# GpSimd forms the low halves of the query weights and of the first ten streamed blocks in a hybrid encoder kernel

## The chip, the core and the metric

The kernel runs on one core of one Trainium2 chip. The metric is the device time of one execution in microseconds (us); lower is better. The time before is the median of three runs.

## The reference, cut to what matters

One encoder block over 512 tokens of width 1024: a mixer (short convolution and pooling) with its output projection, then an expert retrieval with product keys, then a gated input embedding and a last norm. The change lies in the expert retrieval:

```python
def peer_block(xb, w_q, sub_keys, expert_u, expert_v):
    q = (xb @ w_q).reshape(T, PEER_HEADS, 2, PEER_HALF)      # 8 heads, 2 x 128
    s = jnp.einsum('thpd,hpkd->thpk', q, sub_keys)           # 128 keys per half
    sv, si = lax.top_k(s, PEER_TOPK)                         # 16 of 128
    cand = sv[:, :, 0, :, None] + sv[:, :, 1, None, :]       # 256 candidates
    top_s, pos = lax.top_k(cand, PEER_TOPK)                  # 16 of 256
    eidx = jnp.take_along_axis(cidx, pos, axis=-1)           # 16384 experts
    gate = jax.nn.softmax(top_s, axis=-1)
    act = jax.nn.gelu(jnp.einsum('thkd,td->thk', expert_u[eidx], xb))
    return jnp.einsum('thk,thkd->td', gate * act, expert_v[eidx])
```

## The kernel before

**Products of split numbers.** Most matmuls are done in three passes. A float32 operand is split into a high half, a rounded copy that ScalarE writes, and a low half, the remainder, which is a subtraction of two tiles in SBUF. `mm3` and `mm3_pair` then issue high x high, high x low and low x high. `split_ld` (lines 95 to 97) makes both halves, for weight pieces in `piece` (lines 166 to 170: load of 128x2048, high half `wH`, low half `wL`), and `projT` (lines 172 to 177) uses them for a projection onto 256 columns.

**Query stage (lines 498 to 520).** For each of 8 heads `projT` makes the queries of 512 tokens from one piece of `w_q`; the piece of the next head is prepared meanwhile in the other of two buffers (line 501). The scores against the keys go to the tile `s`, and VectorE takes the top 16 of each half there and then (`head`, lines 340 to 352).

**Dense and gathered experts.** For 384 of the 512 tokens the kernel doesn't gather: it streams all 16384 rows of `expert_u` in 128 blocks, multiplies each with all tokens and weights the results by a gate matrix that is zero nearly everywhere. The other 128 tokens (group `ND`) use gathers: GpSimd issues 256 indirect DMAs of 128 rows (`fetch`, lines 534 to 538) and VectorE does the arithmetic (`gather`, lines 545 to 567). Gathers need the indices `eidx` (line 436).

**Block loop (lines 614 to 640).** For block `i` of 76: SP issues the load of block `i + 2` into one of two buffers `uraw` (`u_dma`), ScalarE makes its high half `uH` (`u_h`), VectorE its low half `uL` (`u_l`, lines 582 to 586), three buffers each; TensorE scores block `i` in 24 matmuls of 384 columns; ScalarE applies the gelu, and every fourth block a write `A_d` goes to memory. `prep_u` gives both halves a high priority. Beside this, `main` holds the rest of the retrieval as a list of tasks for VectorE, group `ND` first: candidates, second top-k, decoding of the positions, softmax, `eidx`; then for the other three groups the same and the one-hot products that build the gate matrix, written out as `G_d`. The loop places the tasks in proportion to the blocks done, and gathers from block `G_START` = 10 on at 0.7 per block.

**Order.** From line 237 to line 751 a planner orders the instructions of each engine: it simulates them by priority and by its own estimate of their durations. Line 563 pins the gathers' arithmetic in program order. The first stage and everything from line 752 on (the mixing of `expert_v`) run in the order written.

Of the kernel before, what the change touches and what calls it, by code (L numbers as in the profile page):

```python
# [7 lines left out]
F32 = mybir.dt.float32  # L8
# [5 lines left out]
OP = mybir.AluOpType  # L14
# [34 lines left out]
GGB = 2  # L49
URB = 2  # L50
G_START = 10
G_RATE1 = 0.7
RATES = (1.5, 3.2, 2.9)
MAIN_ORDER = ((ND, 0, 99), (0, 0, 99), (1, 0, 99), (2, 0, 99))
# [6 lines left out]
def block_kernel(ctx: ExitStack, tc: tile.TileContext, x, pT_in, g_cols, w_in, conv_w, pool_w,  # L61
                 pool_scale, w_o, g_ffn, w_q, keysT, u_rows, u_blk, v_rows, g_ple, w_gate, w_proj,
                 g_final, inv_cnt, iota_rep, iota_c, ident_in, out):
    nc = tc.nc
# [27 lines left out]
    gate3 = consts.tile([P, P], F32, name="gate3")  # L92
    xrow = consts.tile([P, D], F32, name="xrow")

    def split_ld(src, hi, lo):
        nc.scalar.activation(hi, src, AF.Copy)
        nc.vector.tensor_tensor(lo, src, hi.bitcast(F32), op=OP.subtract)

    def rsqrt(ms):
        sq = small.tile([P, 1], F32, name="sq")  # L100
# [57 lines left out]
    def piece_dma(w, c0):  # L158
        raw = wpool.tile([P, DC, 256], F32, name="wraw")
        nc.sync.dma_start(raw, w[:, c0:c0 + 256].rearrange("(c p) n -> p c n", p=P))  # L160
        return raw

    def piece_hl():
        return (wpool.tile([P, DC, 256], F32R, name="wH"), wpool.tile([P, DC, 256], F32R, name="wL"))

    def piece(w, c0):
        raw = piece_dma(w, c0)
        hl = piece_hl()
        split_ld(raw, *hl)
        return hl  # L170

    def projT(w, xh, xl):
        ps = [psum.tile([P, T], F32, name="acc", bufs=4) for _ in range(2)]
        for c in range(DC):
            mm3_pair([(ps[b], w[0][:, c, b * P:(b + 1) * P], w[1][:, c, b * P:(b + 1) * P], xh[:, c], xl[:, c])
                      for b in range(2)], c == 0, c == DC - 1)
        return ps
# [18 lines left out]
    pieces = {}  # L196
# [29 lines left out]
    for c in range(DC + LEAD):  # L226
        if c < DC:
            split_ld(raw0[:, c], w0[0][:, c], w0[1][:, c])
            xT_chunk(0, xs, xh, xl, c)
        d = c - LEAD  # L230
        if d >= 0:
            split_ld(raw1[:, d], w1[0][:, d], w1[1][:, d])
            for b in range(2):
                s = slice(b * P, (b + 1) * P)
                mm3(first[b], w0[0][:, d, s], w0[1][:, d, s], xh[:, d], xl[:, d], d == 0, d == DC - 1)
# [36 lines left out]
    for k, pc in enumerate(order):  # L272
        w = pieces.pop(pc)
        if 0 < k < len(order) - 1:
            pieces[order[k + 1]] = piece(w_in, order[k + 1] * 256)
        elif k:
            pieces["o0"] = piece(w_o, 0)
        both = projT(w, xh, xl) if k else first
        for b in range(2):
            ps = both[b]  # L280
            blk = 2 * pc + b
            kind, g = divmod(blk, 4)
            if kind == 3:
                pool_group(g, ps)
            elif kind == 1:
                cbuf[g] = wk.tile([P, T], F32, name="cb")
                nc.scalar.activation(cbuf[g], ps, AF.Copy)
            elif kind == 2:
                z = wk.tile([P, T + 2], F32, name="zb", bufs=1)
                nc.vector.memset(z[:, 0:1], 0.0)  # L290
                nc.vector.memset(z[:, T + 1:], 0.0)
                nc.vector.tensor_tensor(z[:, 1:T + 1], cbuf[g], ps, op=OP.mult)
                y = wk.tile([P, T], F32, name="yb")
                nc.vector.tensor_scalar(y, z[:, 0:T], cw[:, g, 0:1], None, op0=OP.mult)
                nc.vector.scalar_tensor_tensor(y, z[:, 1:T + 1], cw[:, g, 1:2], y, op0=OP.mult, op1=OP.add)
                nc.vector.scalar_tensor_tensor(y, z[:, 2:T + 2], cw[:, g, 2:3], y, op0=OP.mult, op1=OP.add)
                zbuf[g] = y
            else:
                m = wk.tile([P, T], F32, name="cm", bufs=1)
                nc.vector.tensor_tensor(m, zbuf[g], ps, op=OP.mult)  # L300
                split_ld(m, mixH[:, g], mixL[:, g])

    corder = [4, 5, 6, 7, 0, 1, 2, 3]
    for qd in range(4):
        w = pieces.pop("o%d" % qd)
        if qd < 3:
            pieces["o%d" % (qd + 1)] = piece(w_o, (qd + 1) * 256)
        else:
            pieces["q0"] = piece(w_q, 0)
        for t in range(NT):  # L310
            ps = psum.tile([P, T], F32, name="acc", bufs=4)
            ts = slice(t * P, (t + 1) * P)
            for ci, c in enumerate(corder):
                mm3(ps[:, :256], mixH[:, c, ts], mixL[:, c, ts], w[0][:, c], w[1][:, c], ci == 0, ci == DC - 1)
            hs = h[:, t, qd * 256:(qd + 1) * 256]
            nc.vector.tensor_tensor(hs, hs, ps[:, :256], op=OP.add)
# [181 lines left out]
    for hd in range(H):  # L498
        w = pieces.pop("q%d" % hd)
        if hd + 1 < H:  # L500
            pieces["q%d" % (hd + 1)] = piece(w_q, (hd + 1) * 256)
        qb = []
        both = projT(w, xh, xl)
        for b in range(2):
            ps = both[b]
            qs = wk.tile([P, T], F32, name="cb" if b else "yb")
            nc.scalar.activation(qs, ps, AF.Copy)
            qb.append(qs)
        sh_ = wk.tile([P, NT, 2, P], F32, name="s", bufs=3)
        for tp in range(2):  # L510
            ps = psum.tile([P, T], F32, name="tp", bufs=2)
            for ti in range(2):
                for b in range(2):
                    t = 2 * tp + ti
                    o = (2 * ti + b) * P
                    nc.tensor.matmul(ps[:, o:o + P], qb[b][:, t * P:(t + 1) * P], keys[:, 2 * hd + b],  # L516
                                     start=True, stop=True)
            nc.scalar.activation(sh_[:, 2 * tp:2 * tp + 2],
                                 ps.rearrange("p (t b k) -> p t b k", t=2, b=2), AF.Copy)
        for t in (ND, 0, 1, 2):  # L520
            heads[t](hd, sh_[:, t])
# [23 lines left out]
    def gather(n=1, pin=False):  # L545
        for _ in range(n):
            k = done[0]
            if k >= 2 * P:
                return
            done[0] += 1  # L550
            for kk in range(k, min(k + AHEAD_G, 2 * P)):
                if kk not in rows:
                    rows[kk] = fetch(u_rows if kk < P else v_rows, kk % P)
            g = rows[k]
            if k < P:
                ins = nc.vector.scalar_tensor_tensor(g, g, 1.0, xrow, op0=OP.mult, op1=OP.mult,  # L556
                                                     accum_out=act[:, k:k + 1])
            else:
                accg = accs["g"]
                ins = nc.vector.scalar_tensor_tensor(accg, g, gate3[:, k - P:k - P + 1], accg, op0=OP.mult,  # L560
                                                     op1=OP.add)
            if pin:
                tc.keep_in_program_order(ins)
            if k == P - 1:
                nc.sync.dma_start(xrow, h_d[ND])
                nc.scalar.activation(act, act, AF.Gelu_apprx_tanh)
                nc.vector.tensor_tensor(gate3, gate3, act, op=OP.mult)

    ublk, vblk, wblk = {}, {}, {}
# [12 lines left out]
    def u_l(i):  # L582
        if i < NE:
            raw, uh, _ = ublk[i]
            ublk[i][2] = ub.tile([P, DC, P], F32R, name="uL")
            nc.vector.tensor_tensor(ublk[i][2], raw, uh.bitcast(F32), op=OP.subtract)  # L586

    def v_dma(n):
        if n < NE:
# [28 lines left out]
    def prep_u(i):  # L618
        u_dma(i)
        with tc.high_priority(AHEAD):  # L620
            u_h(i)
            u_l(i)
# [3 lines left out]
    for i in range(NB):  # L626
# [9 lines left out]
        while mi < len(main) and spent < (i + 1) * total_m / (NB - SLACK):  # L636
            spent += main[mi][0]
            main[mi][1]()
            mi += 1
        gather(max(0, int((i + 1 - G_START) * G_RATE1) - done[0]), True)  # L640
    phg.close()
# [64 lines left out]
    def quota(r):  # L706
        rate[0] += r
        n = int(rate[0])
        rate[0] -= n
        return n  # L710
# [61 lines left out]
    for m in range(PRE):  # L772
        heldU[m] = acts(NR + m)
        if m == 0:
            for t in range(ND):
                acc[t] = [psum.tile([P, T], F32, name="o%d%d" % (t, hf)) for hf in range(2)]
        u_h(NB + m + 2)
        u_l(NB + m + 2)
        u_dma(NB + m + 4)
        gelu(NR + m, heldU[m])  # L780
    LAST = 3
    left = None
    for n in range(NE - LAST):
        m = n + LAG
        i = n - NS
# [10 lines left out]
        q = quota(r)  # L796
# [23 lines left out]
        if fu:  # L820
            u_l(u_of(m) + 2)
            u_dma(u_of(m) + 4)
# [168 lines left out]
```

## Time and profile before

| what | value |
|---|---|
| median of three runs | 1458.21 us (1457.02 to 1458.67) |
| the profiled execution | 1454.53 us |
| its span on the core | 1452.8 us |
| TensorE busy | 1429.9 us |
| VectorE busy | 1146.7 us |
| ScalarE busy | 621.5 us |
| GpSimd busy | 385.6 us |

The stages by time in the profiled execution: the mixer to about 160 us, the query stage to 278 us, the streamed blocks of the loop to about 650 us, the mixing to about 1400 us, then the tail. "Busy" is the time in which an engine has an instruction in work. A view by stretches gives the same for any part of the span, with the clock that TensorE was granted (1.00 is 2.4 GHz). A view of waits says who waited for whom. Times inside the span count from its start.

### The profile page before, as it was taken

What the parts mean: (1) busy time and instruction counts of PE and PEld (TensorE: products, weight loads), DVE (VectorE), ACT (ScalarE), POOL (GpSimd) and SP (SyncE); (2) the same over time, 40 slices, a digit from 0 to 9 for tenths busy, and PEclk for the clock granted to TensorE, in tenths of its full rate; (3) what the DMA queues carried; (4) which work ended last, traced back from release to release, by engine and by line L of the source; (5) the groups of instructions that cost most, each with busy time, mean ns of one, the idle gap of its engine ahead of it and who ended that gap; (6) DMA issues with size and microseconds to landing.
All of it is one profiled execution on the core that took longest, in us unless ns stands there. A gap on an engine that the chain in (4) does not pass through costs nothing.

```text
span 1452.8 us, 20735 instructions
## 1 busy us (share of the span) xinstructions
PE 1429.9 (98%) x7785; PEld 1270.7 (87%) x7785; DVE 1146.7 (79%) x2206; ACT 621.5 (43%) x928; POOL 385.6 (27%) x260
## 2 busy tenths in 40 slices
PE   8999999999998999999999999999999999999997
PEld 5789888999998999997999999999998888888886
DVE  5644579899998887877999788887887778777765
ACT  5321533344564665663333333333333334443354
POOL 0000000002132132123766555454453112343000
PEclk9999999999999999999999999999999999999999
DMA  8233630047688899898999989998988899998622
GB/s 302 87 94 104 237 117 30 30 166 275 227 286 275 262 316 328 269 312 292 381 351 357 380 321 334 349 346 326 348 318 281 322 341 343 339 336 329 250 69 73
DMA packets 152086, 381.40 MB, mean 263 GB/s; under 512 B 10929, under 2 KB 72113, under 8 KB 151729
## 3 DMA queue, kind: packets, MB, share of 16 engines
q1 hardware_dynamic: 72400, 211.75, 41.3%
q0 software_dynamic: 36864, 134.23, 25.2%
q10 hardware_dynamic: 42720, 34.08, 7.3%
q8 instruction: 61, 1.00, 0.3%
q14 instruction: 41, 0.33, 0.1%
HBM read 339.92 MB, written 40.11 MB: 262 GB/s over the span
## 4 chain that ended last, share of the span: by engine, by line
PE 79%; DVE 7%; issue 5%; DMA 5%; ACT 1%; POOL 1%; ACTq 0%; SPq 0%; POOLq 0%; DVEq 0%
PE o L125 13%; PE o L127 13%; PE o L123 13%; PE acc L125 7%; PE acc L123 7%; PE acc L127 7%; PE u L127 5%; PE u L123 5%; PE u L125 5%; DMA uraw<-in_u_blk 3%; DVE uL L586 2%; DMA G_d<-stage 1%; PE acc L191 1%; POOL gr L536 1%; PE tp L516 1%
## 5 line engine op out<-in xcount | busy, mean ns | idle before, releaser
L536 POOL DMA_INDIRECT gr<-in_u_rows,eidx x128 | 191.5, 1496 | 664.9 <-DVE tsm L390 334.3
L536 POOL DMA_INDIRECT gr<-in_v_rows,eidx x128 | 193.9, 1514 | 279.8 <-DVE xrow L560 270.7
L125 PE MATMUL o<-vL,wH 128*128 128x512 f32 x768 | 237.2, 390 | 1.0 <-DVE vL L604 1.0
L123 PE MATMUL o<-vH,wH 128*128 128x512 f32 x768 | 237.5, 390 | 0.0
L127 PE MATMUL o<-vH,wL 128*128 128x512 f32 x768 | 237.3, 390 | 0.2 <-DVE wL L684 0.2
L123 PE MATMUL acc<-xH,uH 128*128 128x384 f32 x608 | 206.6, 340 | 3.1 <-ACT uH L580 3.1
L598 ACT ACTIVATE vH<-vraw 128x1024 fp32r<-128x1024 f32 x128 | 135.3, 1057 | 168.5 <-PE o L127 94.5
L125 PE MATMUL acc<-xL,uH 128*128 128x384 f32 x608 | 206.8, 340 | 0.0
L127 PE MATMUL acc<-xH,uL 128*128 128x384 f32 x608 | 204.7, 338 | 0.6 <-DVE uL L586 0.6
L604 DVE TENSOR_TENSOR vL<-vraw,vH 128x1024 fp32r<-128x1024 f32 x128 | 156.1, 1220 | 44.5 <-ACT vH L598 44.4
L580 ACT ACTIVATE uH<-uraw 128x1024 fp32r<-128x1024 f32 x128 | 135.2, 1057 | 103.0 <-DMA uraw<-in_u_blk 63.1
L586 DVE TENSOR_TENSOR uL<-uraw,uH 128x1024 fp32r<-128x1024 f32 x128 | 155.7, 1218 | 23.6 <-ACT uH L580 23.6
L125 PEld LDWEIGHTS o<-vL,wH 128*128 128x128 f32 x768 | 144.0, 188 | 32.6 <-DVE vL L604 1.8
L127 PEld LDWEIGHTS o<-vH,wL 128*128 128x128 f32 x768 | 143.9, 188 | 31.3 <-DVE wL L684 1.0
L560 DVE SCALAR_TENSOR_TENSOR xrow<-gr,gate,xrow 128x1024 f32<-128x1024 f32 x128 | 163.6, 1278 | 4.2 <-DMA xrow<-h_d 4.1
L123 PEld LDWEIGHTS o<-vH,wH 128*128 128x128 f32 x768 | 143.3, 188 | 26.7 <-ACT wH L680 0.2
L556 DVE SCALAR_TENSOR_TENSOR gr<-gr,xrow 128x1024 f32<-128x1024 f32 x128 | 155.1, 1217 | 3.7 <-DMA gr<-in_u_rows,eidx 3.6
L127 PE MATMUL u<-xH,uL 128*128 128x384 f32 x416 | 139.6, 336 | 0.0
L123 PE MATMUL u<-xH,uH 128*128 128x384 f32 x416 | 139.5, 335 | 0.0
L125 PE MATMUL u<-xL,uH 128*128 128x384 f32 x416 | 139.3, 335 | 0.0
L123 PEld LDWEIGHTS acc<-xH,uH 128*128 128x128 f32 x608 | 115.2, 189 | 4.2 <-ACT uH L580 4.1
L127 PEld LDWEIGHTS acc<-xH,uL 128*128 128x128 f32 x608 | 115.0, 189 | 1.4 <-DVE uL L586 1.3
(214 smaller groups left out, 2368.1 us busy)
## 6 DMA issues: line engine op xcount, KB each, us to landing
uraw<-in_u_blk SPq DMA_DIRECT2D x128, 512.0 KB, 4.9
vraw<-in_v_rows SPq DMA_DIRECT2D x128, 512.0 KB, 6.0
G_d<-stage ACTq DMA_DIRECT2D x12, 1664.0 KB, 11.2
gq<-G_d SPq DMA_DIRECT2D x26, 768.0 KB, 7.3
A_d<-a ACTq DMA_DIRECT2D x17, 768.0 KB, 5.3
aq<-A_d SPq DMA_DIRECT2D x17, 768.0 KB, 9.3
wraw<-in_w_in SPq DMA_DIRECT2D x8, 1024.0 KB, 5.8
wraw<-in_w_q SPq DMA_DIRECT2D x8, 1024.0 KB, 5.8
```

What stands on the lines that cost most here:

```text
L123: nc.tensor.matmul(ps, lh, rh, start=start, stop=False)
L125: nc.tensor.matmul(ps, lh, rl, start=False, stop=False)
L127: nc.tensor.matmul(ps, ll, rh, start=False, stop=stop)
L191: nc.tensor.matmul(ps, pT[:, c, t * P:(t + 1) * P], wp[hf][:, c], start=c == 0, stop=c == 1)
L516: nc.tensor.matmul(ps[:, o:o + P], qb[b][:, t * P:(t + 1) * P], keys[:, 2 * hd + b], start=True, stop=True)
L536: nc.gpsimd.indirect_dma_start(out=g, out_offset=None, in_=table, in_offset=bass.IndirectOffsetOnAxis(ap=eidx[:, k:k + 1], axis=0))
L556: ins = nc.vector.scalar_tensor_tensor(g, g, 1.0, xrow, op0=OP.mult, op1=OP.mult, accum_out=act[:, k:k + 1])
L560: ins = nc.vector.scalar_tensor_tensor(accg, g, gate3[:, k - P:k - P + 1], accg, op0=OP.mult, op1=OP.add)
L580: nc.scalar.activation(ublk[i][1], ublk[i][0], AF.Copy)
L586: nc.vector.tensor_tensor(ublk[i][2], raw, uh.bitcast(F32), op=OP.subtract)
L598: nc.scalar.activation(vblk[n][1], vblk[n][0], AF.Copy)
L604: nc.vector.tensor_tensor(vblk[n][2], raw, vh.bitcast(F32), op=OP.subtract)
```

## The change

`split_ld` and `piece` take an engine as an argument. In the query stage the low halves of the pieces of heads 1 to 7 are formed by GpSimd in place of VectorE, and so are those of streamed blocks 0 to 9. Nothing else is edited; the planner orders the instructions anew.

```diff
+UPOOL = 10
...
-    def split_ld(src, hi, lo):
+    def split_ld(src, hi, lo, eng=None):
         nc.scalar.activation(hi, src, AF.Copy)
-        nc.vector.tensor_tensor(lo, src, hi.bitcast(F32), op=OP.subtract)
+        (eng or nc.vector).tensor_tensor(lo, src, hi.bitcast(F32), op=OP.subtract)
...
-    def piece(w, c0):
+    def piece(w, c0, eng=None):
         raw = piece_dma(w, c0)
         hl = piece_hl()
-        split_ld(raw, *hl)
+        split_ld(raw, *hl, eng)
         return hl
...
-            pieces["q%d" % (hd + 1)] = piece(w_q, (hd + 1) * 256)
+            pieces["q%d" % (hd + 1)] = piece(w_q, (hd + 1) * 256, nc.gpsimd)
...
-            nc.vector.tensor_tensor(ublk[i][2], raw, uh.bitcast(F32), op=OP.subtract)
+            (nc.gpsimd if i < UPOOL else nc.vector).tensor_tensor(ublk[i][2], raw, uh.bitcast(F32), op=OP.subtract)
```

## Rows read from the trace of the kernel before

Abbreviations: PE is TensorE, PEld its weight loads, DVE VectorE, ACT ScalarE, POOL GpSimd, SPq the queue from which SP issues DMAs.

**Rows 1.** The page's first part: busy us, share of the span, instructions.
```profile
PE 1429.9 (98%) x7785; PEld 1270.7 (87%) x7785; DVE 1146.7 (79%) x2206; ACT 621.5 (43%) x928; POOL 385.6 (27%) x260
```

**Rows 2.** Busy time by stretches: stretch, length, busy (instructions), clock, DMA share, GB/s.
```profile
186.00:276.00 90.00, 90.00 (x450) 75.37 (x449) 79.23 (x454) 26.92 (x36) 0.00 (x0) 1.00 0.16 52
282.00:334.00 52.00, 52.00 (x302) 52.00 (x301) 52.00 (x252) 24.11 (x32) 0.00 (x0) 1.00 0.50 167
340.00:438.00 98.00, 96.98 (x674) 94.74 (x672) 94.67 (x225) 55.19 (x88) 23.86 (x15) 1.00 0.79 265
438.00:480.00 42.00, 37.34 (x253) 35.03 (x251) 36.77 (x49) 22.18 (x40) 10.49 (x7) 0.92 0.86 274
480.00:700.00 220.00, 218.26 (x1523) 205.53 (x1523) 182.79 (x215) 130.85 (x220) 59.31 (x40) 1.00 0.89 299
700.00:1400.00 700.00, 700.00 (x3360) 613.28 (x3359) 561.37 (x709) 263.21 (x363) 287.66 (x191) 1.00 0.89 328
```
The five busy times stand for PE, PEld, DVE, ACT and POOL, in this order.

**Rows 3.** Timeline of PE at 260 us: start, duration, what, idle before.
```profile
260.44 0.63 PE L125 MATMUL acc<-xL,wH 128*128 128x512 f32 x2
260.90 0.63 PE L127 MATMUL acc<-xH,wL 128*128 128x512 f32 x2
```

**Rows 4.** Waits of PE, whole span: us in total, times, longest.
```profile
PE acc L123 <- ACT uH L580: 3.1, 4, 2.1
...
PE acc L127 <- DVE uL L586: 0.6, 1, 0.6
```

**Rows 5.** Busy time by short stretches, around 452 and 468 us.
```profile
450.00:454.00 4.00, 2.99 (x23) 2.64 (x24) 3.43 (x3) 3.55 (x9) 0.20 (x1) 0.85 1.00 292
454.00:458.00 4.00, 4.00 (x19) 4.00 (x18) 4.00 (x7) 0.67 (x1) 0.06 (x1) 0.72 0.97 315
466.00:470.00 4.00, 3.77 (x15) 3.60 (x13) 4.00 (x7) 2.59 (x6) 0.94 (x1) 0.57 0.39 131
```

**Rows 6.** Groups of DVE, 160 to 276 us: busy us, mean ns, idle before.
```profile
L97 DVE TENSOR_TENSOR wL<-wraw,wH 128x2048 fp32r<-128x2048 f32 x7 | 16.0, 2280 | 2.9 <-ACT wH L96 2.9
...
L348 DVE MAX8 tv<-s 128x8 f32<-128x128 f32 x56 | 12.7, 275 | 9.8 <-ACT s L518 9.7
```

**Rows 7.** Instructions on `eidx`: ns min/median/max, first and last start in us.
```profile
L536 POOL DMA_INDIRECT gr<-in_v_rows,eidx x128: 935/1678/4691, 857.5 to 1328.7; - x128
L436 DVE SCALAR_TENSOR_TENSOR eidx<-tij x1: 315/315/315, 333.5 to 333.5; 128x128 int32<-128x128 f32 x1
```

**Rows 8.** Timeline of ACT: high halves of a weight piece and of blocks.
```profile
246.72 1.92 ACT L96 ACTIVATE wH<-wraw 128x2048 fp32r<-128x2048 f32 x1 [3.37 <-PE acc L125]
...
287.27 1.06 ACT L580 ACTIVATE uH<-uraw 128x1024 fp32r<-128x1024 f32 x1 [2.72 <-PE acc L125]
...
291.43 1.06 ACT L580 ACTIVATE uH<-uraw 128x1024 fp32r<-128x1024 f32 x1 [2.72 <-PE acc L125]
...
308.12 1.06 ACT L580 ACTIVATE uH<-uraw 128x1024 fp32r<-128x1024 f32 x1 [0.20 <-ACT a L633]
```

**Rows 9.** Timeline of POOL: its first gather.
```profile
334.72 1.17 POOL L536 DMA_INDIRECT gr<-in_u_rows,eidx  x1 [334.27 <-DVE tsm L390]
```

**Rows 10.** Instructions on `uL`, 170 to 200 us.
```profile
L586 DVE TENSOR_TENSOR uL<-uraw,uH x3: 1222/1224/1225, 176.7 to 183.1; 128x1024 fp32r<-128x1024 f32 x3
```

**Rows 11.** Groups of DVE, 282 to 308 us.
```profile
L586 DVE TENSOR_TENSOR uL<-uraw,uH 128x1024 fp32r<-128x1024 f32 x7 | 8.4, 1205 | 0.0
L365 DVE TENSOR_TENSOR tcv<-tv 128x64 f32<-128x64 f32 (+5 forms) x14 | 2.3, 209 | 0.0
```

**Rows 12.** Block loads (line 574) issued from 276 to 340 us: time to landing.
```profile
DMA to landing us min/median/max: 3.3/3.6/5.2
```

**Rows 13.** Timeline of DVE: the eleventh block's low half.
```profile
311.35 1.22 DVE L586 TENSOR_TENSOR uL<-uraw,uH 128x1024 fp32r<-128x1024 f32 x1
```

**Rows 14.** Block loads issued from 340 to 450 us: ns, first and last start; landing.
```profile
L574 SPq DMA_DIRECT2D uraw<-in_u_blk x22: 327/328/328, 343.6 to 449.4; - x22
...
DMA to landing us min/median/max: 3.3/4.3/10.1
```

## The prediction

> **What bounds the kernel now.** I read the profile from the top down. The page's first part says TensorE: busy 98% of the span, VectorE 79%, GpSimd 27% [rows 1]. A busy share can hide slow matmuls, so the next view is the busy time by stretches. From 186 to 276 us (query projections and key scores) TensorE is busy 90.00 of 90 us, from 282 to 334 us (the first dozen streamed blocks) 52.00 of 52, and from 700 to 1400 us all of it; what it lacks in the middle lies between 340 and 700 us [rows 2]. In the projections the matmuls also follow each other without a gap: two of 512 columns start every 0.46 to 0.47 us [rows 3]. So in the stretches where the change takes work from VectorE, VectorE has 79.23 of 90 and 52.00 of 52 us [rows 2], and yet nobody on TensorE waits for it. The waits of TensorE confirm it: over the whole run 3.1 us for the high half `uH`, and only 0.6 us, once, for a low half `uL` [rows 4].
>
> What can be won is therefore the holes after 340 us. Idle time there is 1.02 us up to 438, 4.66 in 438 to 480, 1.74 from 480 to 700 [rows 2], 7.4 us together. In and behind the largest hole the granted clock falls: 0.85 and 0.72 in two stretches of 4 us, 0.57 in a third [rows 5], which is (0.15 + 0.28 + 0.43) x 4 = 3.4 us of lost speed between the levels of 2.4 and 1.2 GHz. All told 10.8 us hang on this middle part; the largest hole with its clock is 8.1 of them.
>
> **The change part by part.** *Query weights.* Seven subtractions of 128x2048 leave VectorE, 16.0 us busy [rows 6]. TensorE is at full pitch there, so the removal is worth 0 by itself. VectorE carries no backlog out of this stage either: it idles 9.7 us for scores `s` [rows 6], the last time ahead of the last head's top-k. GpSimd gets the same seven. The trace has no GpSimd arithmetic on tiles; its costliest rows are the indirect DMAs of 0.94 to 4.69 us [rows 7]. I bound the new instruction below by VectorE's own 2.28 us and above by twice the longest GpSimd row, 9.4 us, and take about twice VectorE's, 4.6, nearer to the row of the very same shape. What matters is the room. The last weight piece has its high half at 248.6 us (246.72 + 1.92 [rows 8]) and its low half is first read at 260.90 [rows 3]: 12.3 us, more than the upper bound, so TensorE would not wait at either end. Nothing is queued behind these on GpSimd but the blocks' subtractions; its first gather comes at 334.72 [rows 9]. I cost this part at nothing; the cover is that room, and beyond it every us is one of TensorE's.
>
> *First ten blocks.* Three of the ten subtractions lie before 186 us [rows 10], far ahead of their use; the other seven lie between 281 and 309 us, 8.4 us busy [rows 11], 7.9 us of VectorE's time since neighbours overlap by some 0.07 us. GpSimd's price is bounded by 1.2 us below and 4.7 above. Its limit is the loop of the two `uraw` buffers: landing 3.6 us [rows 12], issue some 0.3, high half 1.06 [rows 8], then the low half, which frees the buffer for the next load on SP's queue. Two blocks take 8.32 us on TensorE (high halves at 287.27 and 291.43, 4.16 apart [rows 8]), so the loop keeps pace as long as the low half takes less than 8.32 - 4.96 = 3.3 us. On VectorE it also stands in a queue: the high half that starts at 308.12 ends at 309.18 [rows 8], its low half starts at 311.35 and ends at 312.57 [rows 13], 3.4 us later. GpSimd, with an empty queue, may take over twice VectorE's time and free the buffer no later. I take 2.4 us, again nearest to the same shape. Cost on TensorE: 0; at the upper bound the loop would fall behind by (4.7 - 3.3) / 2 = 0.7 us per block, 4.9 us over seven blocks, of which the three buffers of each half hide about one block's 4.16.
>
> The Trainium skill, GPSIMD Engine Reference, section 3.1, gives 4497 ns on GpSimd for a two-input instruction of 2048 columns, against 2293 ns on VectorE; an estimate from it is 2.25 us for 1024, and by these the sum would be the same. No row here shows GpSimd's; VectorE's 2280 ns agrees.
>
> *What becomes of VectorE's 7.9 us.* VectorE is full from 282 to 334 us and has `eidx` at 333.5 [rows 7]; the first gather follows at 334.72 [rows 9]. Relieved, it could be there 7.9 us earlier. Against that stands its order: the eleventh block's low half stays on VectorE and starts only 2.2 us behind its high half (309.18 to 311.35), so with an unchanged order VectorE soon stands waiting for TensorE's pace; the planner, which sees the freed time, can fill it with later top-k work. Between 2 and 7.9 us I take 5 for the first gather.
>
> *What that is worth.* The gathers feed a pile-up of DMAs behind the large hole. Before they start, a block's load lands in 3.6 us, at most 5.2 [rows 12]; from 343 to 450 us in 4.3, at most 10.1 [rows 14]; around 452 us the DMA engines are at 1.00 and 0.97 [rows 5], where gathers, loads, `G_d` and `A_d` writes meet. Then a high half comes late and the clock falls. Starting the gathers 5 us, about one block, earlier moves them against the writes and lets VectorE catch up less densely. From 0 to the whole 10.8 us could go. I take half of the 1.02 us before 438 (0.5) and somewhat under half of the 8.1 (3.5), nearer the middle because the clock's part falls away as soon as the hole is short: 4.0 us. The profiled execution took 1454.53 us with its span of 1452.8; the sum is made against it, 1450.5, and carried over to the median of the runs, 1458.2, which lies 3.7 above: **1454.2 us**.
>
> **The rivals.** *No change.* TensorE is full in every stretch that is touched, and after 340 us VectorE is busy 97%, 88% and 83% [rows 2] with waits of its own, in which a lead of 5 us is lost again; the holes shift but don't shrink. For it: only 0.6 us of TensorE's waits name a low half [rows 4]. Its form of "it doesn't do what it says": VectorE's order stays as it was, it idles at the eleventh block's low half, and `eidx` comes 2.2 us earlier at most. Time: 1458.2 plus or minus 2.9.
>
> *Slower: the pile-up grows.* The place is 340 to 600 us. A block takes about 5.0 us there (22 loads between 343.6 and 449.4 [rows 14]), so the loop of two buffers bears a landing of 10.1 - 0.3 - 1.06 - 1.2 = 7.5 us; the longest is already 10.1 [rows 14]. It decides when two such landings follow each other, because gathers that come earlier fall on a `G_d` write. A second hole like the one in 438 to 480 costs 8.1 us, 1466; half of one 1462. Against it: the amount of data is unchanged and there is one such hole in 220 us now.
>
> *Slower: GpSimd and VectorE hinder each other.* From 282 to 308 us VectorE's two-input work other than the low halves is small, the additions for the candidates 2.3 us [rows 11] and a few comparisons and products. If each of these waited for a whole GpSimd subtraction, seven of 2.4 us would put up to 16.8 us on VectorE in place of 7.9; it decides when the waits pass 7.9 us, 1.1 per subtraction. Then the first gather comes up to 8.9 us later, the catch-up is denser, and half a large hole is added: 1462. SBUF — State Buffer in the Trainium skill, section "Who interferes with whom", says that such a VectorE instruction and a GpSimd one that reads SBUF block each other, the later waiting for the whole of the earlier. No row here shows it, since GpSimd reads no tiles beside VectorE before.
>
> **How the numbers follow.** Faster through the middle part: 0.44, forecast 1454.2, its own range 1447.5 (all 10.8 us) to 1455.3. No change: 0.33. Pile-up: 0.16. Hindering: 0.07. The bound of 0.2%, 2.9 us, is about what a measurement of this kernel can tell from no change. The range that should hold 8 in 10 goes from 1447 to 1464: all the holes below, and above three quarters of a second one. So faster 0.44, same 0.33, slower 0.23.
>
> **What would show it.** In the profile after: GpSimd subtractions of under 3.3 us (1024) and under 9.4 us (2048), TensorE still 90 of 90 and 52 of 52 us busy, the first gather near 329 us, the idle time of 438 to 480 us about halved, and a clock above 0.92 there. It is wrong if TensorE idles before 330 us, if VectorE's two-input instructions grow beside GpSimd's, if the first gather is no earlier than 334 us, or if a hole of over 4 us stands elsewhere between 340 and 700 us.

## The result, and the profile after

The changed kernel takes 1468.53 us (median of nine runs, 1463.60 to 1474.27); the kernel before, measured beside it, 1456.93 us (median of nine). The ratio is 1.0094, with a 95% interval of 1.0077 to 1.0112: slower by about 12 us where a gain of 4 us was forecast, and above the forecast range. The profiled execution took 1468.38 us with a span of 1466.6, 13.8 us above that of before.

Busy time by stretches in the kernel after (stretch, length, busy time of PE, PEld, DVE, ACT and POOL with instructions, clock, DMA share, GB/s), to be laid beside [rows 2]:

```profile
186.00:276.00 90.00, 90.00 (x450) 75.33 (x449) 65.95 (x448) 26.43 (x36) 28.85 (x7) 1.00 0.17 54
282.00:334.00 52.00, 45.03 (x241) 44.39 (x240) 52.00 (x238) 19.11 (x26) 16.64 (x7) 0.93 0.36 122
308.00:334.00 26.00, 19.03 (x91) 18.39 (x90) 26.00 (x103) 9.79 (x14) 5.43 (x2) 0.87 0.34 112
340.00:438.00 98.00, 92.56 (x627) 89.82 (x626) 94.90 (x240) 53.09 (x84) 25.96 (x16) 0.97 0.78 262
438.00:480.00 42.00, 42.00 (x307) 41.02 (x306) 40.23 (x51) 26.51 (x46) 9.11 (x6) 1.00 0.95 307
480.00:700.00 220.00, 215.58 (x1513) 204.60 (x1512) 169.89 (x194) 127.83 (x215) 52.82 (x34) 0.99 0.85 285
700.00:1400.00 700.00, 699.87 (x3355) 613.10 (x3354) 565.24 (x706) 263.07 (x357) 298.56 (x197) 1.00 0.91 333
```

In the query stage TensorE is as full as before. The large hole of 438 to 480 us is gone: 42.00 of 42 at a clock of 1.00, where [rows 2] has 37.34 at 0.92. But between 308 and 334 us, a stretch in which TensorE was full, it now idles 7.0 us at a clock of 0.87, and 340 to 438 us has lost 4.4 us more than before. From 276 to 700 us TensorE idles 16.8 us against 7.4, and the clock takes some 6.8 us against 3.4 (an estimate: the missing part of the granted clock times the length of the stretch; for the kernel after 0.13 x 26 in 308 to 334, 0.07 x 26 in 334 to 360 and 0.02 x 78 in 360 to 438). That makes 12.8 of the 13.8 us; the rest lies within the rounding of the clock.

Waits of PE over the whole span (us in total, times, longest), the counterpart of [rows 4]:

```profile
PE acc L128 <- DVE uL L587: 7.8, 3, 5.0
...
PE g L471 <- ACT stage L478: 3.7, 3, 2.9
PE acc L124 <- ACT uH L581: 2.6, 1, 2.6
PE acc L128 <- POOL uL L587: 2.0, 1, 2.0
```

TensorE waited 0.6 us for a low half before; now it waits 9.8 us, mostly for low halves that VectorE still forms.

GpSimd's prices are the estimated ones. A group of POOL from 160 to 276 us (busy us, mean ns of one | idle before), and the instructions on `uL` from 278 to 334 us (ns min/median/max):

```profile
L98 POOL TENSOR_TENSOR wL<-wraw,wH 128x2048 fp32r<-128x2048 f32 x7 | 32.2, 4607 | 200.4 <-ACT wH L97 200.4
```

```profile
L587 POOL TENSOR_TENSOR uL<-uraw,uH x7: 2387/2397/3301, 280.6 to 310.6; 128x1024 fp32r<-128x1024 f32 x7
```

The cause begins on VectorE. Timeline of POOL and of DVE while GpSimd subtracts beside the top-k (start, duration, what, idle before):

```profile
284.42 2.39 POOL L587 TENSOR_TENSOR uL<-uraw,uH 128x1024 fp32r<-128x1024 f32 x1 [1.46 <-ACT uH L581]
288.58 2.39 POOL L587 TENSOR_TENSOR uL<-uraw,uH 128x1024 fp32r<-128x1024 f32 x1 [1.77 <-ACT uH L581]
296.94 2.41 POOL L587 TENSOR_TENSOR uL<-uraw,uH 128x1024 fp32r<-128x1024 f32 x1 [1.49 <-ACT uH L581]
307.33 6.10 POOL L587 TENSOR_TENSOR uL<-uraw,uH 128x1024 fp32r<-128x1024 f32 x2 [7.98 <-ACT uH L581]
```

```profile
284.56 2.33 DVE L366 TENSOR_TENSOR tcv<-tv 128x64 f32<-128x64 f32 x1
...
289.28 1.72 DVE L359 COPY tdf<-tf 128x16 f16<-128x16 f16 x1
...
296.98 2.40 DVE L359 COPY tdf<-tf 128x16 f16<-128x16 f16 x1
...
308.45 2.73 DVE L417 TENSOR_TENSOR tmul<-tmul 128x1024 f16<-128x1024 f16 x1
311.10 2.58 DVE L395 TENSOR_TENSOR gate<-tts,tsm 128x128 f32<-128x128 f32 x1
```

A copy of 16 columns takes 2.40 us. It starts at 296.98, just behind GpSimd's start at 296.94, and both end within 0.03 us of each other (299.35 and 299.38). The addition at 284.56 does the same with the subtraction of 284.42. Each such instruction stands until GpSimd's whole subtraction is done; VectorE starts nothing else meanwhile (its next instruction starts at 299.29), so everything behind it stands as well. The view calls VectorE busy meanwhile: 52.00 of 52 us says nothing of the loss, only the duration of one instruction of one shape does.

Groups of DVE by shape, 278.5 to 334.3 us of the kernel after (busy us, mean ns of one | idle):

```profile
L359 DVE COPY tdf<-tf 128x16 f16<-128x16 f16 x3 | 4.3, 1423 | 0.0
L417 DVE TENSOR_TENSOR tmul<-tmul 128x1024 f16<-128x1024 f16 x3 | 4.1, 1353 | 0.0
L366 DVE TENSOR_TENSOR tcv<-tv 128x64 f32<-128x64 f32 x6 | 3.7, 611 | 0.0
...
L395 DVE TENSOR_TENSOR gate<-tts,tsm 128x128 f32<-128x128 f32 x1 | 2.6, 2582 | 0.0
...
L400 DVE COPY tmx<-tts 128x8 f32<-128x8 f32 x2 | 1.8, 923 | 0.0
```

In the kernel before the same five shapes take 162, 692, 225, 410 and 162 ns in this stretch. The difference is 3 x 1.26 + 3 x 0.66 + 6 x 0.39 + 2.17 + 2 x 0.76 = 11.8 us. Against it, VectorE has ten low halves fewer ahead of `eidx` (seven on GpSimd, three that the new order places behind it): 10 x 1.13 = 11.3 us. So the lead is spent before it reaches the gathers:

```profile
L537 POOL DMA_INDIRECT gr<-in_u_rows,eidx x5: 935/1348/2780, 334.9 to 342.4; - x5
...
L437 DVE SCALAR_TENSOR_TENSOR eidx<-tij x1: 280/280/280, 334.4 to 334.4; 128x128 int32<-128x128 f32 x1
```

These are the instructions on `eidx` up to 345 us in the kernel after (ns min/median/max, first and last start). It stands at 334.4 us and the first gather at 334.9, where [rows 7, 9] have 333.5 and 334.72.

That alone would make it no faster. The holes before 334 us come with an order that had counted on the lead; what this order costs in all is measured further down. Timeline of ACT, then PE and DVE, kernel after:

```profile
297.26 1.28 ACT L386 ACT_TABLE_LOAD   x1
305.99 0.31 ACT L386 ACTIVATE tts<-tts 128x128 f32<-128x128 f32 x1 [7.45 <-DVE tts L385]
306.20 1.05 ACT L581 ACTIVATE uH<-uraw 128x1024 fp32r<-128x1024 f32 x1
```

```profile
310.68 0.44 PE L128 MATMUL acc<-xH,uL 128*128 128x384 f32 x1 [1.96 <-POOL uL L587]
...
325.86 0.69 PE L128 MATMUL acc<-xH,uL 128*128 128x384 f32 x1 [5.01 <-DVE uL L587]
```

```profile
324.61 1.20 DVE L587 TENSOR_TENSOR uL<-uraw,uH 128x1024 fp32r<-128x1024 f32 x1
```

ScalarE's exponential of group `ND` stands one place earlier than before, ahead of the high half of block 8. It waits 7.45 us for a held-up VectorE (2.37 us in the kernel before), and `uH` of block 8 waits behind it until 306.20; the low halves of blocks 8 and 9 then come back to back, 6.10 us at 307.33, and TensorE waits 1.96 us. The low half of block 10, VectorE's first, starts at 324.61 instead of at 311.35 [rows 13] and costs 5.01 us. Around these the clock falls.

### The profile page after: what moved, and what is told of

Read it like the earlier page. It is cut to its first block, busy times and chain, and to the rows that moved or that the text cites. A ratio compares the mean times of both kernels' runs of the same rounds, so it can differ in the third digit from the quotient of the medians.

```text
span 1466.6 us, 20738 instructions
## 1 busy us (share of the span) xinstructions
PE 1433.5 (98%) x7785; PEld 1274.3 (87%) x7785; DVE 1134.5 (77%) x2189; ACT 621.9 (42%) x928; POOL 449.2 (31%) x277
## 4 chain that ended last, share of the span: by engine, by line
PE 72%; DVE 13%; DMA 8%; issue 3%; ACT 2%; ACTq 1%; POOL 0%; SPq 0%; DVEq 0%; POOLq 0%
PE o L126 10%; PE o L128 10%; PE o L124 10%; PE acc L128 8%; PE acc L124 8%; PE acc L126 8%; PE u L128 5%; PE u L124 5%; PE u L126 5%; DMA uraw<-in_u_blk 4%; DMA tH<-in_w_gate 3%; DVE uL L587 2%; DVE vL L605 1%; DMA G_d<-stage 1%; PE tp L517 1%
## 5 line engine op out<-in xcount | busy, mean ns | idle before, releaser
L128 PE MATMUL acc<-xH,uL 128*128 128x384 f32 x608 | 208.3, 343 | 9.8 <-DVE uL L587 7.8
L587 DVE TENSOR_TENSOR uL<-uraw,uH 128x1024 fp32r<-128x1024 f32 x118 | 143.7, 1219 | 32.7 <-ACT uH L581 31.8
## 6 DMA issues: line engine op xcount, KB each, us to landing
G_d<-stage ACTq DMA_DIRECT2D x12, 1664.0 KB, 10.8
```

The source lines that it names most:

```text
L128: nc.tensor.matmul(ps, ll, rh, start=False, stop=stop)
L587: (nc.gpsimd if i < UPOOL else nc.vector).tensor_tensor(ublk[i][2], raw, uh.bitcast(F32), op=OP.subtract)
```

## Which part of the change costs: three runs

**The query weights alone**, blocks as before:

```diff
-UPOOL = 10
+UPOOL = 0
```

> The changed kernel with GpSimd taking the seven query weight pieces alone; all blocks stay on VectorE; the order is that of the kernel before. Theories 'hold' and 'order': 1454 to 1460, as before, with VectorE 13 to 16 us less busy between 160 and 276 us and TensorE 90 of 90 us busy from 186 to 276. Theory 'query weights': over 1460, with longer VectorE instructions beside the 4.6 us ones of GpSimd.

Measured: 1454.76 us, ratio to the kernel before 1.0001 (0.9983 to 1.0018).

**The query weights and three early blocks:**

```diff
-UPOOL = 10
+UPOOL = 3
```

> The changed kernel with GpSimd taking the query weights and blocks 0 to 2 alone; blocks 3 to 9 stay on VectorE. TensorE's, ScalarE's and SP's order is that of the kernel before but for a few places. Theory 'hold': GpSimd does nothing between 254 and 334 us, so nothing of VectorE is held up where it is full; the query stage has no slack to win; 1454 to 1460, no difference from before. Theory 'order': the same, since the order is the same. Theory 'query weights' (the seven long subtractions of 4.6 us on GpSimd cost as well): 1460 or more.

Measured: 1453.94 us, ratio 0.9993 (0.9975 to 1.0010). The first gather comes at 334.9 us, with the weights alone at 334.6: as before.

**The ten blocks alone**, weights on VectorE:

```diff
-            pieces["q%d" % (hd + 1)] = piece(w_q, (hd + 1) * 256, nc.gpsimd)
+            pieces["q%d" % (hd + 1)] = piece(w_q, (hd + 1) * 256)
```

> Blocks 0 to 9 on GpSimd, the query weights back on VectorE; the rest and TensorE's order as in the changed kernel. If only the seven subtractions beside the second top-k cost something, as the runs with the weights alone (1454.8) and with the weights and three early blocks (1453.9) suggest, it takes 1466 to 1471 us, TensorE loses 10.5 us between 308 and 360 us again, and VectorE is 79 of 90 us busy from 186 to 276 us. If the weights on GpSimd contribute (a backlog or a hindrance that only shows together with the blocks), it takes 1455 to 1463 us.

Measured: 1468.66 us, ratio 1.0088 (1.0056 to 1.0120). Its stretch of 308 to 334 us:

```profile
308.00:334.00 26.00, 17.45 (x88) 16.81 (x87) 26.00 (x103) 9.68 (x14) 5.21 (x2) 0.87 0.35 112
```

What follows: weights and early blocks are worth nothing either way, to within the 0.2% of these intervals, and the whole loss belongs to the seven subtractions beside the second top-k or to the order that the planner makes with them. The next runs separate the two.

## Held instructions or the order: three runs

In these three the order of TensorE, ScalarE and VectorE is that of the changed kernel, and only GpSimd's work on blocks differs.

**GpSimd only writes.** For blocks 3 to 9 it fills the low halves with zeros, which leaves the subtraction out of their scores:

```diff
+            if 3 <= i < UPOOL:
+                nc.gpsimd.memset(ublk[i][2].bitcast(F32), 0.0)
```

> The changed kernel, but GpSimd fills the low halves of blocks 3 to 9 with zeros in place of subtracting; that part of the scores is left out. TensorE, ScalarE, VectorE and SP have exactly the changed kernel's order. Theory 'hold' (GpSimd's subtractions, which read tiles, hold up VectorE's instructions: 11.8 us of lengthening against 11.3 us saved, and the order reckoned with the saving): without the reads VectorE's short instructions are back at 0.15 to 0.7 us, the first gather comes near 326 us in place of 334.9, the holes of 2.0 and 5.0 us on TensorE before 330 us are gone, and the time is 1450 to 1458. Theory 'order' (the planner's new order is bad in itself, whatever VectorE does): the holes stay and the time is 1465 to 1471.

Measured: 1456.15 us, ratio 1.0007 (0.9990 to 1.0025). Groups of DVE in the same stretch as above, and the first gathers:

```profile
L366 DVE TENSOR_TENSOR tcv<-tv 128x64 f32<-128x64 f32 x6 | 1.3, 214 | 0.0
...
L359 DVE COPY tdf<-tf 128x16 f16<-128x16 f16 x3 | 0.5, 165 | 0.0
L395 DVE TENSOR_TENSOR gate<-tts,tsm 128x128 f32<-128x128 f32 x1 | 0.4, 411 | 0.0
```

```profile
L537 POOL DMA_INDIRECT gr<-in_u_rows,eidx x8: 933/1516/2770, 322.8 to 343.6; - x8
```

Nothing is held, the first gather comes 12 us earlier than in the kernel before, and 12.4 us of the loss are gone. Both holes on TensorE before 330 us are gone as well. But against the kernel before nothing is won: in this order a lead of 12 us, more than I had hoped for, is needed to come out even. The holes have moved (this profiled execution took 1460.11 us, 4 us above the median of its runs):

```profile
308.00:360.00 52.00, 48.00 (x262) 47.00 (x261) 50.39 (x179) 20.86 (x27) 15.55 (x10) 0.95 0.64 228
...
480.00:700.00 220.00, 211.56 (x1456) 199.09 (x1455) 166.92 (x192) 122.87 (x206) 51.88 (x35) 0.99 0.84 282
```

TensorE idles 8.4 us from 480 to 700, where [rows 2] has 1.7; 7.5 us of it are waits for `stage`, ScalarE's copies of the gate matrix.

The run changes one thing more. A write reads neither the raw block nor its high half, so the raw buffer comes free sooner: the first block load after 276 us is issued at 280.3 us, against 283.0 in the kernel after. How much of the 12.4 us this is worth wasn't tested apart; TensorE's waits for GpSimd's low halves were 2.0 us in the kernel after. The slices, next, still read both.

**The subtractions in four slices of 256 columns:**

```diff
+USLICE = 4
...
+            if i < UPOOL:
+                for k in range(0, DC, DC // USLICE):
+                    s = slice(k, k + DC // USLICE)
+                    nc.gpsimd.tensor_tensor(ublk[i][2][:, s], raw[:, s], uh[:, s].bitcast(F32), op=OP.subtract)
```

> The changed kernel with each block's subtraction on GpSimd cut into four of 256 columns; the order on TensorE, ScalarE, VectorE and SP is exactly the changed kernel's. Theory 'hold', the hold lasting for one GpSimd instruction: one that VectorE meets holds it for at most about 0.7 us in place of 2.4, so the lengthening falls from 11.8 to some 4 us, the first gather comes near 329 us, the holes before 330 us shrink from 7 to 0 to 3 us, and the time is 1456 to 1464. If the hold lasts as long as GpSimd has work, or if only the order counts: 1465 to 1472.

Measured: 1462.28 us, ratio 1.0051 (1.0032 to 1.0069). A slice takes 0.74 us, so a held instruction loses less of VectorE's time; the first gather comes at 327.4 us, about midway between the whole subtractions (334.9) and the writes (322.8), and the time lies midway as well.

**GpSimd copies**, one tile read in place of two (for blocks 3 to 9 the low half is a copy of the raw block, so their scores come out other than the reference's):

```diff
+            if 3 <= i < UPOOL:
+                nc.gpsimd.tensor_copy(ublk[i][2], raw)
```

> For blocks 3 to 9 GpSimd only copies the raw block into the low half's tile instead of subtracting: one tile read instead of two (this leaves the subtraction out of these blocks' scores). The order on TensorE, ScalarE and VectorE is that of the changed kernel, so only the kind of GpSimd's instruction differs. If any GpSimd instruction that reads tiles holds VectorE up, the copy of 16 columns, the additions for the candidates and the gate's product are lengthened by about the time of GpSimd's copy (1 to 2.4 us each), the first gather comes at 328 us or later and it takes 1460 to 1468 us. If only one with two tiles as inputs does, VectorE's instructions have their usual lengths, the first gather comes near 323 us and it takes 1455 to 1458 us.

Measured: 1459.79 us, ratio 1.0032 (1.0014 to 1.0049), between the two expectations, so the time doesn't decide. The timelines do. The same pair of VectorE's additions falls beside GpSimd's instruction here and in the run with writes; first the copy:

```profile
295.77 1.05 POOL L588 CAST uL<-uraw 128x1024 fp32r<-128x1024 f32 x1 [3.11 <-PE acc L128]
```

```profile
296.33 0.76 DVE L366 TENSOR_TENSOR tcv<-tv 128x128 f32<-128x128 f32 x2
```

then the write:

```profile
295.85 0.96 POOL L588 MEMSET uL<- 128x1024 f32 x1 [3.20 <-PE acc L128]
```

```profile
296.30 0.41 DVE L366 TENSOR_TENSOR tcv<-tv 128x128 f32<-128x128 f32 x2
```

Beside the copy the pair takes 0.76 us, beside the write 0.41. One input on GpSimd is enough to hold VectorE; a copy of 1.05 us merely holds it for less time, and few instructions fall on it (first gather at 323.9 us). My rival that it takes two inputs on GpSimd falls.

## The order: five runs

One instruction pinned: ScalarE's exponential of group `ND` keeps its place in the program's order. The planner then comes to another order for everything (in the trace `eidx` is VectorE's 834th instruction instead of its 877th), so this is a change of the order as a whole, not of one place.

**Pinned, whole subtractions:**

```diff
-            nc.scalar.activation(ts, ts, AF.Exp)
+            ins = nc.scalar.activation(ts, ts, AF.Exp)
+            if t == ND:
+                tc.keep_in_program_order(ins)
```

> The changed kernel with one instruction pinned: ScalarE's exponential of group ND comes behind the high half of block 8, as in the kernel before, and VectorE's low half of block 10 has 24 instructions fewer ahead of it. GpSimd's subtractions stay whole. If the lengthened VectorE instructions alone cost the time, they are still there (11 us more on VectorE) and it takes 1464 to 1469 us. If they cost it only together with an order that counts on a lead which isn't there, it takes 1455 to 1460 us: ScalarE doesn't idle 7.45 us near 300 us, TensorE idles under 3 us from 308 to 334 us, and the first gather still comes at 333 us or later.

Measured: 1453.77 us, ratio 0.9984 (0.9969 to 0.9998). The time is even below what the theory "only together with the order" gave, but two of its details are wrong: VectorE's instructions are still held (the three copies of 16 columns 1428 ns each), yet the first gather comes at 326.7 us, and TensorE still idles 4.9 us from 308 to 334. What is gone are the later holes:

```profile
308.00:360.00 52.00, 45.23 (x246) 44.39 (x245) 50.97 (x210) 18.89 (x24) 10.94 (x9) 0.93 0.61 218
360.00:480.00 120.00, 119.75 (x867) 116.87 (x867) 117.78 (x211) 75.58 (x124) 25.82 (x18) 1.00 0.82 273
480.00:700.00 220.00, 220.00 (x1539) 208.74 (x1537) 186.57 (x222) 130.83 (x219) 61.58 (x43) 1.00 0.92 309
```

**Pinned, four slices**, both edits:

```diff
+USLICE = 4
...
+                tc.keep_in_program_order(ins)
```

> Both repairs at once: ScalarE's exponential of group ND pinned behind the high half of block 8, and each of GpSimd's block subtractions cut into four of 256 columns. If the held-up instructions and the order are the two causes, it takes 1453 to 1458 us, about the time of the kernel before, since a lead of the gathers was worth nothing when GpSimd only wrote (1456.2). If the lead is worth something once the holes before 340 us are gone, it takes 1447 to 1452 us. If the slices' loss (7.5 us) has another place than these two, it takes 1460 to 1464 us.

Measured: 1448.97 us, ratio 0.9959 (0.9943 to 0.9975), first gather at 323.0 us. This version is faster than both kernels.

**Pinned, eight slices of 128 columns:**

```diff
-USLICE = 4
+USLICE = 8
```

> The pinned run with each of GpSimd's block subtractions cut into eight of 128 columns instead of four of 256; same order. If the length of the single GpSimd instruction sets what VectorE loses, the held instructions grow by under 0.4 us each and it takes 1446 to 1449 us. If GpSimd's own time then limits (eight with their fixed part come to more than the 3.3 us that the loop of two raw buffers bears), TensorE idles again for its low halves and it takes 1451 to 1458 us.

Measured: 1447.08 us, ratio 0.9946 (0.9928 to 0.9963), first gather at 322.3 us. Half the slice gains little more; the two intervals overlap. Timeline of POOL in this run, sixteen slices for blocks 8 and 9, and the slices of blocks 3 to 9 one by one (ns min/median/max):

```profile
301.30 13.42 POOL L593 TENSOR_TENSOR uL<-uraw,uH 128x128 fp32r<-128x128 f32 x16 [0.55 <-ACT uH L584]
```

```profile
L593 POOL TENSOR_TENSOR uL<-uraw,uH x56: 457/463/1446, 280.3 to 314.1; 128x128 fp32r<-128x128 f32 x56
```

That is 6.7 us for a block, twice the 3.3 us that the two raw buffers bear; the five blocks before took 3.4 to 3.6 us, a little above it too. Most of the 6.7 isn't the number of slices: single slices grow from 0.46 to as much as 1.45 us there, beside VectorE's products of 2048 columns, and the four slices of the run before took 9.81 us for the same two blocks. Nor is it shown that this limits the kernel: TensorE idles 4.8 us from 308 to 360, with four slices 5.4.

**Pinned, GpSimd only writes** (blocks 3 to 9 without their subtraction):

```diff
+                nc.gpsimd.memset(ublk[i][2].bitcast(F32), 0.0)
...
+                tc.keep_in_program_order(ins)
```

> The order of the two pinned runs on TensorE, ScalarE and VectorE, but GpSimd only writes zeros into the low halves of blocks 3 to 9 (this leaves the subtraction out of these blocks' scores): nothing is held, at the same order. With the whole subtractions (1453.8) and the slices (1449.0) it makes a row of three. If what VectorE is held is the whole difference between them, the first gather comes at 319 us or earlier and it takes 1443 to 1448 us. If a lead beyond the sliced run's 11.7 us brings nothing more, it takes 1448 to 1452 us. If holes move as in the run with writes in the unpinned order, it takes 1453 to 1458 us.

Measured: 1441.91 us, ratio 0.9916 (0.9892 to 0.9940), first gather at 317.1 us, a little faster than any of the expectations. TensorE is full all through the middle:

```profile
308.00:360.00 52.00, 52.00 (x303) 51.96 (x302) 51.52 (x213) 26.32 (x33) 11.40 (x9) 1.00 0.68 238
360.00:480.00 120.00, 119.76 (x888) 116.60 (x887) 117.13 (x209) 74.54 (x126) 25.61 (x17) 1.00 0.85 282
480.00:700.00 220.00, 220.00 (x1511) 208.32 (x1511) 187.80 (x224) 129.40 (x215) 67.44 (x47) 1.00 0.94 317
```

**The kernel before with the same pin**, no low half on GpSimd:

```diff
+                tc.keep_in_program_order(ins)
```

> The kernel before, all low halves on VectorE, with the same instruction of ScalarE (the exponential of group ND) pinned as in the two runs of 1453.8 (pinned, whole subtractions) and 1449.0 (pinned, in four slices). If those owe their time to GpSimd's share together with the order, this one stays at the time of the kernel before, 1453 to 1459 us, with its first gather at 333 us or later and a hole behind it. If the pinned order makes the gain by itself, whoever forms the low halves, it takes 1447 to 1451 us.

Measured: 1455.73 us, ratio 1.0027 (1.0007 to 1.0046), first gather at 332.4 us, 5.6 us idle from 480 to 700. The pin by itself gains nothing. (Its order is a third one, since VectorE's work is another.)

Laid side by side, median times in us:

| GpSimd on blocks 3 to 9 | changed order | pinned order | difference |
|---|---|---|---|
| subtracts, whole | 1468.5 | 1453.8 | 14.7 |
| subtracts in four slices | 1462.3 | 1449.0 | 13.3 |
| only writes | 1456.2 | 1441.9 | 14.3 |
| whole minus writes | 12.3 | 11.9 | |

Both columns lose about 12 us between writes and whole subtractions, close to the 11.8 us for which VectorE was held in the kernel after; every row loses about 14 us to the changed order. The runs come from several series, in which the kernel before took 1454.3 to 1456.9 us. Taken as ratios to it, the rows lose 16.0, 13.4 and 13.2 us and the columns 12.7 and 9.9, each uncertain by some 3 to 4 us. Within that the two costs simply add up. So the order's cost doesn't hang on the missing lead: with the lead there, when GpSimd only writes, it's as large.

This also says what the lead is worth. With writes in place of whole subtractions the first gather comes 12.1 us earlier in the changed order and 9.6 us in the pinned one, and the time falls by 12.3 and 11.9 us (an upper price, since the same edit frees the raw buffers sooner). From the kernel before, then, some 12 us could be won (ratio 0.9916); the changed order takes about as much away again (1.0007), and the held instructions cost some 12 more (1.0094).

What stays open is which place of that order costs the 14 us. The runs in it show TensorE idle 4.4 to 8.4 us from 480 to 700 us, the four with GpSimd's share in the pinned order 0.00, and in that stretch the waits for `stage` (3.7 us with whole subtractions, 5.4 with four slices, 7.5 with writes) name the queue; moving single places of it wasn't tried.

## Why the prediction was wrong, point by point

- *What bounds the kernel, and the pile-up.* The bound is right, and worth more than stated: all the holes were put at 10.8 us, and with nothing held in the pinned order the kernel gains 12.4 with no hole left. The forecast that the hole of 438 to 480 us shrinks came true in the kernel after by luck, since it has no earlier gather. Why it went is open: the busy share of the DMA engines is 1.11 and 1.04 there in two stretches of 4 us from 454 us, and TensorE is full, so full DMA engines alone don't make the hole.
- *Query weights.* Right. GpSimd took 4607 ns for one, against my 4.6 us; TensorE stayed at 90.00 of 90, and the run without this part has the same time.
- *The price of a block on GpSimd.* Right in the median (2397 ns against 2.4 us), and below the 3.3 us of the buffer loop. The Trainium skill, GPSIMD Engine Reference, section 3.1, gives 4497 ns for 2048 columns; the trace agrees with 4607 ns.
- *What becomes of VectorE's 7.9 us.* This is the step that failed. I let VectorE keep its speed beside GpSimd and put 5 us on the first gather; it lost 11.8 us and the gather came 0.2 us later than before. The mechanism stood among the rivals as "GpSimd and VectorE hinder each other", but with a chance of 0.07, because I counted only VectorE's two-input work (2.3 us in 282 to 308 [rows 11]) and took its small share of busy time for a small risk. What counts is whether one such instruction falls into each subtraction, not how long it is: VectorE starts an instruction every 0.1 to 0.3 us there, and one of the held kinds met each of the seven subtractions, the first for 0.3 us only. I also left out the copies of one input, 5 of the 11.8 us. The rival's deciding point, 1.1 us per subtraction, was passed with 11.8 / 7 = 1.7.
- *Its bounds, and the order.* My price for that rival was 1462, from half a large hole. I saw the lost lead. But the new order itself is a second term that failed: the sum has what it does to ScalarE and TensorE at nothing, without a reason, and the runs price it at about 14 us. The exponential ahead of block 8's high half and the low half of block 10 far back are the places seen before 334 us. I named the danger of the order in the other direction only (an order unchanged, with VectorE idle). A slip in the sum: the lower end of the forecast's own range, 1458.2 less 10.8, is 1447.4 and not 1447.5.
- *What the lead is worth.* About right. I gave 4.0 us for a lead of 5, 0.8 for each; the runs give 1.0 and 1.2 in the two orders, as an upper price. That the run with writes in the changed order ends at the time of the kernel before (1456.2) is not "no change": its gain pays for the order. In the pinned order GpSimd's share is worth 13.8 us when nothing is held (1455.7 to 1441.9, the former with an order of its own).
- *The rules in the Trainium skill.* The Trainium skill, SBUF — State Buffer, section "Who interferes with whom", says that a VectorE instruction with two inputs in SBUF contends with a GpSimd one that reads SBUF and not with one that only writes, and that some copies of one input contend too; whoever starts second waits for the whole of the first. The traces agree at each point: 2.33 us for an addition of 64 columns, 0.41 us for the pair beside a write, 2.40 us for the copy. It was on the table and had a price; I gave it too small a chance because no row of the kernel before could show it.

## What to carry to other kernels

Before moving tile work to GpSimd, count for each of its instructions whether VectorE will meet it with an instruction of a kind that is held, however short, and price that meeting at GpSimd's whole remaining duration; short GpSimd instructions make each meeting cheaper. Where a planner orders the code, a change of its assumed durations is a second change: test the order apart from the work, for instance with the same order and harmless work in place of the moved one, and check what else the harmless work sets free. A gain and a loss of the same size can hide each other: the run with writes alone looked like "no change", and only the second order showed that it was over 12 us won and as much lost.

## What the runs showed of the hardware

GpSimd is held too when VectorE is first. In the kernel after, GpSimd's subtraction of block 8 starts at 307.33 and takes 3.30 us, the longest of its seven. VectorE's product of 2048 columns started 0.12 us before it and keeps its usual length:

```profile
307.21 1.21 DVE L414 TENSOR_TENSOR tmul<-tcmp,tdf 128x2048 f16<-128x2048 f16 x1
```

A chain of VectorE instructions holds it longer. In the pinned run with whole subtractions, POOL and DVE near 305 us:

```profile
305.37 4.10 POOL L589 TENSOR_TENSOR uL<-uraw,uH 128x1024 fp32r<-128x1024 f32 x1 [1.50 <-ACT uH L583]
```

```profile
305.18 0.53 DVE L366 TENSOR_TENSOR tcv<-tv 128x32 f32<-128x32 f32 x4
...
305.99 1.22 DVE L410 TENSOR_TENSOR tcmp<-tpf,steps 128x2048 f16<-128x2048 f16 x1
307.25 3.31 DVE L416 TENSOR_TENSOR tmul<-tcmp,tdf 128x2048 f16<-128x2048 f16 x1
```

The subtraction starts 0.19 us behind the additions and grows from 2.40 to 4.10 us, as if it began when the comparison of 305.99 ended. The product behind takes 3.31 us instead of 1.21 and ends 1.1 us after the subtraction. The instructions of the top-k itself (MAX8, MATCH_REPLACE8, FIND_INDEX8 on 128 columns) take 0.28 to 0.29 us beside GpSimd's 4.6 us subtractions, 0.27 to 0.28 in the kernel before. VectorE has nothing else to do from 186 to 276 us once the low halves are gone, so the query stage could bear the change.
